# Sums of squares emitted a step behind their squares around an output projection, and two cache copies issued later

## The chip, the cores and the metric

The kernel runs on one core of a Trainium2 chip. It is measured in device microseconds (us) of one execution, lower being better. Five engines work side by side: TensorE (PE) multiplies matrices, VectorE (DVE) and ScalarE (ACT) work elementwise, GpSimd (POOL) does some elementwise work, and SyncE (SP) issues most DMAs. ACT issues some DMAs too. Each engine runs its own instructions in the order in which the program lists them, and waits on semaphores for the others.

## The reference

One inference step of one decoder layer, on a prompt of 1024 tokens and on 8 short sequences of 4 tokens (1056 columns in all, model width 1024, float32):

```python
h = rmsnorm(x, g_pre)
p = h @ w_in                       # split among three mixers and three gates
za, conv_a_new = causal_dwconv(a_c * a_in, conv_a_prev, conv_a_w)
ya = a_b * za                      # mixer A: gated convolution
yb, k_new, v_new = window_attn_...(q, k, v, ...)   # mixer B: window attention
yc = chunk_spatial_gate(c_u, rmsnorm(c_v, g_v), w_s, b_s)   # mixer C
g = sigmoid(gates)
merged = g[0] * (ya @ w_ba) + g[1] * (yb @ w_bb) + g[2] * (yc @ w_bc)
x = x + rmsnorm(merged @ w_o, g_post)
up = rmsnorm(x, g_pre_f) @ w_up
upc, ffn_new = causal_dwconv(up, ffn_prev, conv_f_w, conv_f_b)
fa, fb = split(upc, 2)
x = x + rmsnorm((silu(fa) * fb) @ w_down, g_post_f)
```

Here `rmsnorm(z, g)` is `z * rsqrt(mean(z*z) + eps) * g` over the 1024 features. The key and value caches of the short sequences are also returned, shifted by four rows: 124 old rows of each of 8 sequences are copied from input to output, for keys (`wk`) and values (`wv`).

## The kernel before

Features lie on the 128 partitions (8 tiles of 128, index `n`), tokens along the free axis. The 1056 columns are cut into three chunks `c` of 352 (`CW`). Every float32 product is made of three passes: an operand is split into a rounded part and a remainder (`copy` on ACT, line 91, then `sub` on DVE, line 97), and `products` multiplies hi by hi, hi by lo and lo by hi. Weights come by DMA on SP's queue into `raw` (three buffers), and are split into `wh`/`wl` or into a place in `Y`.

The program runs in this order. First the input `x` is loaded into `M`; for each chunk ACT squares it (`sq`, `acc`, line 434), DVE adds the squares, `rstd_of` multiplies the sum by `ones` on PE (`aux<-ones,acc`), POOL raises it to the power -1/2 (`rs`, line 311), PE spreads it over the partitions (line 320), and DVE and ACT make `H`, the normalized operand. Then come the input projections, the mixers, and the branch stage: eight branch tiles `n`, each with three products, whose results are multiplied by the gates `sig` (loaded back from DRAM into 12 buffers) in `evac_y`. Then the output projection, the feed-forward up projections, the down projections, and the end.

In the output projection the chunks come one after another. For each of the 8 tiles of a chunk, `evac_o` lets ACT store the product times a gain in `M` and square it; DVE adds the squares into `acc`. When a chunk is done, a generator `chain(c, ...)` does the rest of that chunk a step at a time, while PE works on the next chunk: `rstd_of(acc)`; then for the tiles in pairs a multiplication by `rs` and an addition of the input `xr` (both DVE, `M<-M,rs` and `M<-M,xr`), a DMA of the new `x` to DRAM (`x2d`), two squares on ACT (`acc2` for the first pair, `sq` for the others) and two additions into `acc2` on DVE; then `rstd_of(acc2)` and the splitting into `H`. PE's order is written out by hand for the whole kernel, and DVE's order for this stage is the order in which the code emits it (`manual_schedule`). The other engines are put in order by a scheduler that works with its own estimate of time.

In the trace the sum of `chain` is called `acc`, its squares `sq` and, for the third chunk, both are `cz`; the third chunk's first sum lies in `R`. A DMA uses one of eight semaphores in turn, and waits until the DMA that used it last has landed.

Of the kernel before, what the change touches and what calls it, by code (L numbers as in the profile page):

```python
# [17 lines left out]
P = 128  # L18
# [4 lines left out]
CW = 352  # L23
# [16 lines left out]
def body(tc, i, o):  # L40
# [3 lines left out]
    with top, tc.manual_schedule(engines={mybir.EngineType.PE}):  # L44
# [48 lines left out]
        def tt(out, a, b, op, eng=dve):  # L93
            return eng.tensor_tensor(out, a, b, op=op)  # L94
# [764 lines left out]
        with tc.tile_pool(name="pb", bufs=1) as pb:  # L859
            sig = {}  # L860

            def load_g(n):
                for b in (0, 2, 1):
                    for c in CHUNKS:
                        s = sig[b, n, c] = pb.tile([P, CW], F32, name="sig", tag="sig", bufs=12)
                        nc.sync.dma_start(s, sigd[:, 8 * b + n, cc(c)])

            def evac_y(b, n):
                def f(c, ps):
                    m, s = M8[:, n, cc(c)], sig.pop((b, n, c))  # L870
                    if b == 0:
                        tt(m, ps, s, ALU.mult)
                        return
                    tt(s, ps, s, ALU.mult)
                    last = tt(m, m, s, ALU.add, pool)
                    if n == 1 and b == 1 and c == 2:
                        with tc.issue_after(last.ins):
                            nc.scalar.dma_start(o["wk"], i["ck"][:, 4:, :])
                            nc.scalar.dma_start(o["wv"], i["cv"][:, 4:, :])
                    if b == 1:  # L880
                        copy(H[:, n, cc(c)], m)
                        sub(H[:, 8 + n, cc(c)], m, f32(H[:, n, cc(c)]))
                return f

            for n in range(8):
                load_g(n)
                unit(2, lambda k: Y[:, 12 + k, :], lambda k: Y[:, 14 + k, :], evac_y(0, n))
                unit(2, lambda k: Y[:, 8 + k, :], lambda k: Y[:, 10 + k, :], evac_y(2, n))
                unit(4, lambda k: Y[:, k, :], lambda k: Y[:, 4 + k, :], evac_y(1, n))
# [1 line left out]

        pcs = ExitStack()
        pc = open_pool(pcs, "pc", bufs=1)
        sums = {}

        def evac_o(n, acc):
            def f(c, ps):
                act.activation(M8[:, n, cc(c)], ps, AF.Identity, scale=g_post[:, n : n + 1])
                if c == 2:
                    if n == 0:  # L900
                        act.activation(acc, ps, AF.Square)
                        return
                    sq = pc.tile([P, CW], F32, name="sq", bufs=1)
                    act.activation(sq, ps, AF.Square)
                    tt(acc, acc, sq, ALU.add)
                elif n < 2:
                    act.activation(acc[:, n, :], ps, AF.Square)
                else:
                    if n % 2 == 0:
                        sums[c] = pc.tile([P, 2, CW], F32, name="sq2", bufs=1)  # L910
                    act.activation(sums[c][:, n % 2, :], ps, AF.Square)
                    if n % 2:
                        tt(acc, acc, sums[c], ALU.add)
            return f

        def load_xr(c, n, xr, queue=nc.sync):
# [2 lines left out]
        def chain(c, acc, rs, xr, acc2, sq, fill):  # L919
# [2 lines left out]
                return [None] * n  # L922

            queue = nc.sync if c < 2 else nc.scalar
            yield
            spread = rstd_of(acc, rs)
            next(fill, None)
            yield from wait(2)
            spread()
            for n in range(0, 8, 2):  # L930
                m = M8[:, n : n + 2, cc(c)]
                tt(m, m, rs.unsqueeze(1).to_broadcast([P, 2, CW]), ALU.mult)
                tt(m, m, xr[n // 2], ALU.add)
                queue.dma_start(x2d[:, n : n + 2, cc(c)], m)
                if c == 2 and n < 4:
                    load_xr(c, n + 4, xr[n // 2], queue)
                for q in range(2):
                    if n == 0:
                        act.activation(acc2[:, q, :], m[:, q, :], AF.Square)
                    else:  # L940
                        act.activation(sq[q], m[:, q, :], AF.Square)
                if n:
                    for q in range(2):
                        tt(acc2[:, q, :], acc2[:, q, :], sq[q], ALU.add)
                yield
            yield from wait(3)
            spread = rstd_of([acc2[:, 0, :], acc2[:, 1, :]], R[:, cc(c)])
            next(fill, None)
# [23 lines left out]
        for c in CHUNKS:  # L972
            if c < 2:
                xr = [pc.tile([P, 2, CW], F32, name="xr", bufs=4) for _ in range(4)]
                for n in range(0, 8, 2):
                    load_xr(c, n, xr[n // 2])
            acc = pc.tile([P, 2, CW], F32, name="acc") if c < 2 else R[:, cc(2)]
            for n in range(8):
                for _ in products(8, Hhi, Hlo, evac_o(n, acc), (c,), pieces=wow + 2 * n):
                    for step in steps:  # L980
# [4 lines left out]
            if c < 2:  # L985
                pair = lambda name, **kw: pc.tile([P, 2, CW], F32, name=name, **kw)
                sq = pair("sq3")
                steps.append(chain(c, acc, pc.tile([P, CW], F32, name="rs"), xr, pair("acc2"),
                                   [sq[:, 0, :], sq[:, 1, :]], iter(())))
        pcs.close()  # L990
        pw.close()
        taken[0] = upw + 8
# [332 lines left out]
```

## Time and profile before

| | |
|---|---|
| time, median of 3 runs (lowest, highest) | 1483.58 us (1479.41, 2008.34) |
| profiled execution, its own time | 1479.45 us |
| span of its core, first to last instruction | 1477.7 us |
| PE busy, share of the span | 1430.0 us, 97% |
| DVE, ACT, POOL busy | 61%, 45%, 17% |

The span is counted from the first instruction to the last. All places below are given in us from its start: the input phase up to about 48, the branch stage from about 545 to 642, the output projection from 642 to 745, the up projections from there on. PE is the engine that is busy nearly all the time, so a change of the time has to be looked for where PE stands still or is slow.

### The profile page before, as it was taken

How to read it: one execution, taken by the hardware profiler on the slowest of the kernel's cores; microseconds unless marked ns; L12 is line 12 of the kernel's file. 1: busy time of each engine (PE TensorE's matmuls, PEld its weight loads, DVE VectorE, ACT ScalarE, POOL GpSimd, SP SyncE). 2: the span in 40 equal slices, each digit the busy share in tenths (PEclk: the TensorE clock that was granted, in tenths of full speed). 3: DMA queues.
4: the chain of work that ended last, by engine and by line, in shares of the span. 5: the costliest groups of instructions: out<-in, count | busy, mean ns of one | idle time of the engine just before them, and what ended most of it. 6: DMA issues, size and time to landing. Idle time of an engine off the chain costs nothing.

```text
span 1477.7 us, 25715 instructions
## 1 busy us (share of the span) xinstructions
PE 1430.0 (97%) x10163; PEld 1419.4 (96%) x10163; DVE 903.0 (61%) x1615; ACT 659.0 (45%) x1347; POOL 248.4 (17%) x319
## 2 busy tenths in 40 slices
PE   4899999999999999999899999999999999999997
PEld 4899999999999989999899999999999999999997
DVE  6844445324777546655578877778777783453546
ACT  5444444435776322244446554455544574121333
POOL 2100000012455215520002212222122110000000
PEclk9999999999999999999999999999999999999999
DMA  6222333211001136643232222221222174231315
GB/s 232 77 90 98 103 109 110 92 48 44 30 23 44 60 107 186 189 140 108 82 110 73 78 75 82 85 87 66 72 84 77 54 259 152 73 109 44 86 38 154
DMA packets 77833, 141.40 MB, mean 96 GB/s; under 512 B 8256, under 2 KB 34816, under 8 KB 77696
## 3 DMA queue, kind: packets, MB, share of 16 engines
q1 hardware_dynamic: 64816, 110.77, 23.7%
q10 hardware_dynamic: 12896, 28.98, 5.2%
q8 instruction: 80, 1.31, 0.4%
q14 instruction: 41, 0.34, 0.1%
HBM read 105.58 MB, written 35.16 MB: 95 GB/s over the span
## 4 chain that ended last, share of the span: by engine, by line
PE 90%; DVE 4%; ACT 2%; issue 2%; POOL 1%; DMA 1%; ACTq 0%; SPq 0%; POOLq 0%; DVEq 0%
PE mm L100 54%; PE wb L100 20%; PE aux L100 13%; DVE M L94 1%; POOL rs L311 1%; PE sp L100 1%; ACT M L700 1%; PE aux L713 1%; DMA M<-in_x 1%; DVE M L694 0%; DMA raw<-in_wu 0%; DVE acc L94 0%; DVE Y L97 0%; ACT Y L91 0%; PE aux L320 0%
## 5 line engine op out<-in xcount | busy, mean ns | idle before, releaser
L100 PE MATMUL mm<-Y,wh 128*128 128x264 f32 (+1 forms) x1824 | 363.8, 295 | 0.0
L100 PE MATMUL mm<-H,wh 128*128 128x352 f32 (+1 forms) x1568 | 354.3, 313 | 1.5 <-DVE Y L97 0.9
L100 PEld LDWEIGHTS mm<-Y,wh 128*128 128x128 f32 x1824 | 292.6, 188 | 0.0
L100 PE MATMUL mm<-Y,wl 128*128 128x264 f32 (+1 forms) x912 | 269.4, 295 | 0.0
L100 PEld LDWEIGHTS mm<-H,wh 128*128 128x128 f32 x1568 | 261.6, 188 | 2.5 <-PE aux L100 1.1
L100 PE MATMUL mm<-H,wl 128*128 128x352 f32 (+1 forms) x784 | 243.7, 311 | 0.0
L100 PEld LDWEIGHTS mm<-Y,wl 128*128 128x128 f32 x912 | 171.8, 188 | 0.0
L100 PE MATMUL wb<-H,wh 128*128 128x264 f32 (+1 forms) x720 | 147.7, 298 | 0.0
L91 ACT ACTIVATE wh<-M 128x512 fp32r<-128x512 f32 x126 | 79.5, 631 | 152.8 <-PE aux L100 65.9
L100 PEld LDWEIGHTS mm<-H,wl 128*128 128x128 f32 x784 | 147.3, 188 | 0.0
L91 ACT ACTIVATE wh<-raw 128x512 fp32r<-128x512 f32 (+1 forms) x98 | 58.3, 594 | 169.2 <-PE mm L100 110.6
L1062 DVE SCALAR_TENSOR_TENSOR cz<-U,cst,cz 128x1072 f32<-128x1072 f32 x88 | 113.8, 1330 | 11.0 <-ACT cz L1060 11.0
L100 PEld LDWEIGHTS wb<-H,wh 128*128 128x128 f32 x720 | 116.4, 188 | 0.0
L100 PE MATMUL mm<-H,Y 128*128 128x352 f32 x624 | 107.2, 331 | 2.6 <-DVE H L97 2.6
L100 PE MATMUL wb<-H,wl 128*128 128x264 f32 (+1 forms) x360 | 107.3, 298 | 0.0
L97 DVE TENSOR_TENSOR wl<-M,wh 128x512 fp32r<-128x512 f32 x126 | 86.5, 686 | 32.8 <-ACT wh L91 32.8
L100 PEld LDWEIGHTS mm<-H,Y 128*128 128x128 f32 x624 | 103.1, 192 | 3.0 <-DVE H L97 3.0
L97 DVE TENSOR_TENSOR wl<-xraw,wh 128x512 fp32r<-128x512 f32 x70 | 48.5, 693 | 90.3 <-ACT wh L91 89.8
L311 POOL TENSOR_TENSOR rs<-rs,nhalf 88x4 f32<-88x4 f32 (+2 forms) x12 | 23.6, 1964 | 392.5 <-DVE rs L310 392.5
L94 DVE TENSOR_TENSOR M<-mm,M 128x352 f32<-128x352 f32 (+3 forms) x79 | 39.5, 506 | 76.2 <-PE mm L100 76.2
L94 DVE TENSOR_TENSOR M<-M 128x512 f32<-128x512 f32 (+1 forms) x88 | 69.5, 790 | 27.1 <-DMA M<-in_wu 26.3
L97 DVE TENSOR_TENSOR wl<-raw,wh 128x512 fp32r<-128x512 f32 (+1 forms) x72 | 53.0, 737 | 51.7 <-ACT wh L91 51.7
(222 smaller groups left out, 2635.8 us busy)
## 6 DMA issues: line engine op xcount, KB each, us to landing
M<-in_wu SPq DMA_DIRECT2D x72, 256.0 KB, 2.6
sig<-sigd SPq DMA_DIRECT2D x72, 176.0 KB, 2.9
y2d<-cz ACTq DMA_DIRECT2D x22, 528.0 KB, 2.8
sigd<-M ACTq DMA_DIRECT2D x40, 264.0 KB, 3.4
xraw<-in_win SPq DMA_DIRECT2D x40, 256.0 KB, 2.7
raw<-in_wd SPq DMA_DIRECT2D x40, 256.0 KB, 2.6
raw<-in_win SPq DMA_DIRECT2D x39, 256.0 KB, 2.6
Y<-y2d SPq DMA_DIRECT2D x14, 528.0 KB, 6.6
```

The source lines that it names most:

```text
L91: act.activation(out, in_, AF.Copy)
L94: return eng.tensor_tensor(out, a, b, op=op)
L97: eng.tensor_tensor(out, a, b, op=ALU.subtract)
L100: pe.matmul(out, lhsT, rhs, start=start, stop=stop, skip_group_check=more)
L311: pool.tensor_tensor(v, v, nhalf[:bs, :nb], op=ALU.pow)
L700: act.activation(s[:, h, :], s[:, h, :], AF.Exp, bias=ng[:, h : h + 1], scale=SCALE, accum_out=l[:, h : h + 1])
L713: pe.transpose(pt[:, h * P : (h + 1) * P], s[:, h, kb * P : (kb + 1) * P], ident)
L1062: dve.scalar_tensor_tensor(z, u[:, s : s + CONV], cwf[:, f, s : s + 1], z, ALU.mult, ALU.add)
```

## The change

It has two parts. In the output projection the addition of a square is not emitted next to the square any more but one step later: `evac_o` squares every tile by itself into one of three `sq` buffers, appends its addition to a list `late`, and first empties that list of the tile before (`flush`); `chain` adds the squares of a pair of tiles (`add_squares`) after the next pair's DVE work. The sum `acc` of the first two chunks is 352 wide, where it was two halves of 352 that were added up at the end. And the two DMAs that copy the cache rows are tied to the copy of branch tile 1 into `H` on ACT, where they were tied to an addition on POOL.

```diff
-                    last = tt(m, m, s, ALU.add, pool)
-                    if n == 1 and b == 1 and c == 2:
-                        with tc.issue_after(last.ins):
-                            nc.scalar.dma_start(o["wk"], i["ck"][:, 4:, :])
-                            nc.scalar.dma_start(o["wv"], i["cv"][:, 4:, :])
+                    tt(m, m, s, ALU.add, pool)
                     if b == 1:
-                        copy(H[:, n, cc(c)], m)
+                        last = act.activation(H[:, n, cc(c)], m, AF.Copy)
+                        if n == 1 and c == 2:
+                            with tc.issue_after(last.ins):
+                                nc.scalar.dma_start(o["wk"], i["ck"][:, 4:, :])
+                                nc.scalar.dma_start(o["wv"], i["cv"][:, 4:, :])
...
+        late = []
+
+        def flush():
+            while late:
+                tt(*late.pop())
 
         def evac_o(n, acc):
             def f(c, ps):
                 act.activation(M8[:, n, cc(c)], ps, AF.Identity, scale=g_post[:, n : n + 1])
...
+                if n == 0:
+                    act.activation(acc, ps, AF.Square)
+                    return
+                sq = pc.tile([P, CW], F32, name="sq", bufs=3)
+                act.activation(sq, ps, AF.Square)
+                flush()
+                late.append((acc, acc, sq, ALU.add))
             return f
...
             queue = nc.sync if c < 2 else nc.scalar
+            flush()
             yield
             spread = rstd_of(acc, rs)
...
+            def add_squares():
+                for q in range(2):
+                    tt(acc2[:, q, :], acc2[:, q, :], sq[q], ALU.add)
+
             for n in range(0, 8, 2):
...
+                if n > 2:
+                    add_squares()
                 for q in range(2):
-                    if n == 0:
-                        act.activation(acc2[:, q, :], m[:, q, :], AF.Square)
-                    else:
-                        act.activation(sq[q], m[:, q, :], AF.Square)
-                if n:
-                    for q in range(2):
-                        tt(acc2[:, q, :], acc2[:, q, :], sq[q], ALU.add)
+                    act.activation(sq[q] if n else acc2[:, q, :], m[:, q, :], AF.Square)
                 yield
+            add_squares()
```

PE and POOL keep their order; on ACT, DVE and SP it moves at the following places. At the head of ACT's program, before:

```order
L333 DMA cst<-in_cst 128x80
L91 ACT_TABLE_LOAD
L91 ACTIVATE warm<-nhalf 128x4
L878 DMA out_wk<-in_ck 8x15872
L879 DMA out_wv<-in_cv 8x15872
L91 ACTIVATE Y<-raw 128x512
L434 ACTIVATE acc<-M 128x704
```

and after, in the branch stage, where the next product's weights are split between the copies of a tile into `H`:

```order
L91 ACTIVATE wh<-raw 128x512
L877 ACTIVATE H<-M 128x352
L880 DMA out_wk<-in_ck 8x15872
L881 DMA out_wv<-in_cv 8x15872
L91 ACTIVATE wh<-raw 128x256 x2
```

The copies were ACT's fourth and fifth instruction, ahead of all work on `x`; now they stand behind the third `H<-M` of branch tile 1. The rest of the input phase has the same order on ACT.

DVE, while PE works on the third chunk and `chain` on the second, before (`acc_7599` is that chain's `acc2`, `R` the third chunk's first sum, `Y<-raw,Y` the splitting of weights for the up projections):

```order
L94 TENSOR_TENSOR M<-M,rs 128x2x352
L94 TENSOR_TENSOR M<-M,xr 128x2x352
L94 TENSOR_TENSOR acc_7599<-acc_7599,sq_7597 128x352 x2
L94 TENSOR_TENSOR R<-R,sq 128x352
L94 TENSOR_TENSOR M<-M,rs 128x2x352
L94 TENSOR_TENSOR M<-M,xr 128x2x352
L94 TENSOR_TENSOR acc_7599<-acc_7599,sq_7597 128x352 x2
L97 TENSOR_TENSOR Y<-raw,Y 128x512 x2
L94 TENSOR_TENSOR M<-M,rs 128x2x352
L94 TENSOR_TENSOR M<-M,xr 128x2x352
L94 TENSOR_TENSOR acc_7599<-acc_7599,sq_7597 128x352 x2
L94 TENSOR_TENSOR R<-R,sq 128x352
```

and after (`acc_7613` is the same sum):

```order
L94 TENSOR_TENSOR M<-M,rs 128x2x352
L94 TENSOR_TENSOR M<-M,xr 128x2x352
L94 TENSOR_TENSOR R<-R,sq 128x352
L94 TENSOR_TENSOR M<-M,rs 128x2x352
L94 TENSOR_TENSOR M<-M,xr 128x2x352
L94 TENSOR_TENSOR acc_7613<-acc_7613,sq_7611 128x352 x2
L97 TENSOR_TENSOR Y<-raw,Y 128x512 x2
L94 TENSOR_TENSOR M<-M,rs 128x2x352
L94 TENSOR_TENSOR M<-M,xr 128x2x352
L94 TENSOR_TENSOR acc_7613<-acc_7613,sq_7611 128x352 x2
L94 TENSOR_TENSOR R<-R,sq 128x352
L94 TENSOR_TENSOR acc_7613<-acc_7613,sq_7611 128x352 x2
```

Each pair of additions has moved behind the multiplication and addition of the next pair of tiles; the last two pairs of additions now stand next to each other, with one addition into `R` between them.

ACT at the same place, before:

```order
L941 ACTIVATE sq_7597<-M 128x352 x2
L898 ACTIVATE M<-mm,cst 128x352
L91 ACTIVATE Y<-raw 128x512
L941 ACTIVATE sq_7597<-M 128x352 x2
L91 ACTIVATE wh<-raw 128x512
```

and after:

```order
L941 ACTIVATE sq_7611<-M 128x352 x2
L902 ACTIVATE M<-mm,cst 128x352
L907 ACTIVATE sq<-mm 128x352
L91 ACTIVATE Y<-raw 128x512
L91 ACTIVATE wh<-raw 128x512
L941 ACTIVATE sq_7611<-M 128x352 x2
```

The last two squares of the chain stood behind one splitting of weights, and now stand behind two, and behind the square of the product that PE has just finished.

## Rows read from the trace of the kernel before

**Rows 1.** The page, busy time of each engine.

```profile
PE 1430.0 (97%) x10163; PEld 1419.4 (96%) x10163; DVE 903.0 (61%) x1615; ACT 659.0 (45%) x1347; POOL 248.4 (17%) x319
```

**Rows 2.** Waits of PE: us in total, times, longest.

```profile
PE aux L100 <- DVE acc L94: 19.7, 4, 14.5
```

**Rows 3.** Timeline, input phase: start, duration, engine, line, instructions, [idle before <-releaser].

```profile
0.81 0.40 SPq L135 DMA_DIRECT2D raw<-in_win  x1
...
1.34 1.26 ACTq L878 DMA_DIRECT2D out_wk<-in_ck  x1
...
4.03 0.63 ACT L91 ACTIVATE Y<-raw 128x512 fp32r<-128x512 f32 x1 [1.26 <-DMA raw<-in_win]
...
10.06 0.79 ACT L434 ACTIVATE acc<-M 128x704 f32<-128x704 f32 x1 [5.40 <-DMA M<-in_x]
...
12.58 0.79 ACT L434 ACTIVATE sq<-M 128x704 f32<-128x704 f32 x1 [0.16 <-DMA M<-in_x]
...
14.50 2.51 PE L100 MATMUL aux<-ones,acc 128*88 128x1 f32 x16 [14.50 <-DVE acc L94]
```

**Rows 4.** Busy time by stretch, ending with PE clock, DMA share, GB/s.

```profile
4.00:10.00 6.00, 0.00 (x0) 0.00 (x0) 0.86 (x2) 0.63 (x1) 0.00 (x0) 1.00 0.76 265
...
16.00:22.00 6.00, 3.74 (x24) 3.39 (x25) 4.68 (x9) 4.67 (x9) 1.66 (x1) 1.00 1.06 396
```

**Rows 5.** Waits of SP's queue in the input phase.

```profile
SPq L135 <- DMA out_wk<-in_ck: 1.8, 1, 1.8
```

**Rows 6.** Timeline of PE, output projection and first up projections.

```profile
691.72 1.51 PE L100 MATMUL aux<-ones,acc 128*88 128x1 f32 x16
...
707.41 0.76 PE L100 MATMUL aux<-ones,acc 128*88 128x1 f32 x8 [0.24 <-DVE acc L94]
708.03 4.11 PE L100 MATMUL wb<-H,Y 128*128 128x352 f32 x24
...
730.75 2.56 PE L100 MATMUL aux<-ones,acc 128*88 128x1 f32 x16 [4.68 <-DVE acc L94]
733.17 5.93 PE L100 MATMUL wb<-H,Y 128*128 128x352 f32 x24
...
768.18 1.64 PE L100 MATMUL aux<-ones,cz 128*88 128x1 f32 x16 [0.64 <-issue]
```

**Rows 7.** Busy time by stretch, behind PE's wait; PE clock third from the end.

```profile
731.00:738.00 7.00, 7.00 (x35) 7.00 (x35) 2.44 (x7) 2.64 (x5) 1.00 (x1) 0.56 0.25 75
```

**Rows 8.** Timeline of DVE while PE works on the third chunk.

```profile
717.78 0.89 DVE L94 TENSOR_TENSOR M<-M,xr 128x704 f32<-128x704 f32 x1
720.99 0.96 DVE L94 TENSOR_TENSOR acc<-acc,sq 128x352 f32<-128x352 f32 x2 [2.32 <-ACT sq L941]
721.87 0.52 DVE L94 TENSOR_TENSOR R<-R,sq 128x352 f32<-128x352 f32 x1
...
724.74 0.96 DVE L94 TENSOR_TENSOR acc<-acc,sq 128x352 f32<-128x352 f32 x2 [0.62 <-ACT sq L941]
725.62 1.29 DVE L97 TENSOR_TENSOR Y<-raw,Y 128x512 fp32r<-128x512 f32 x2
...
730.08 0.96 DVE L94 TENSOR_TENSOR acc<-acc,sq 128x352 f32<-128x352 f32 x2 [1.45 <-ACT sq L941]
```

**Rows 9.** Timeline of ACT at the same place.

```profile
729.03 0.63 ACT L91 ACTIVATE Y<-raw 128x512 fp32r<-128x512 f32 x1 [3.50 <-DMA raw<-in_wu]
729.57 0.87 ACT L941 ACTIVATE sq<-M 128x352 f32<-128x352 f32 x2
```

**Rows 10.** Timeline of SP's queue, branch stage and output projection.

```profile
571.87 1.62 SPq L866 DMA_DIRECT2D sig<-sigd  x3
...
726.37 0.96 SPq L135 DMA_DIRECT2D raw<-in_wu  x2
```

**Rows 11.** The tile sig in the branch stage: its loads, from issue to landing.

```profile
DMA to landing us min/median/max: 2.3/2.8/4.7
```

**Rows 12.** Timeline of DVE, start of branch tile 3: its second use of sig.

```profile
583.29 0.51 DVE L94 TENSOR_TENSOR M<-wb,sig 128x352 f32<-128x352 f32 x1
```

More of the change, by code (lines that the diff above doesn't have):

```diff
@@ L893, in body @@
         pc = open_pool(pcs, "pc", bufs=1)
-        sums = {}
+        late = []
+        def flush():
+            while late:
+                tt(*late.pop())
         def evac_o(n, acc):
@@ L898, in f @@
                 act.activation(M8[:, n, cc(c)], ps, AF.Identity, scale=g_post[:, n : n + 1])
-                if c == 2:
-                    if n == 0:
[L901 to L907, printed above, removed]
-                else:
[L909 to L913, printed above, removed]
+                if n == 0:
[5 more added lines that the diff above has]
+                late.append((acc, acc, sq, ALU.add))
             return f
@@ L936, in chain @@
                     load_xr(c, n + 4, xr[n // 2], queue)
+                if n > 2:
+                    add_squares()
                 for q in range(2):
-                    if n == 0:
-                        act.activation(acc2[:, q, :], m[:, q, :], AF.Square)
-                    else:
-                        act.activation(sq[q], m[:, q, :], AF.Square)
-                if n:
-                    for q in range(2):
-                        tt(acc2[:, q, :], acc2[:, q, :], sq[q], ALU.add)
+                    act.activation(sq[q] if n else acc2[:, q, :], m[:, q, :], AF.Square)
                 yield
+            add_squares()
             yield from wait(3)
@@ L976, in body @@
                     load_xr(c, n, xr[n // 2])
-            acc = pc.tile([P, 2, CW], F32, name="acc") if c < 2 else R[:, cc(2)]
+            acc = pc.tile([P, CW], F32, name="acc") if c < 2 else R[:, cc(2)]
             for n in range(8):
@@ L987, in body @@
                 sq = pair("sq3")
-                steps.append(chain(c, acc, pc.tile([P, CW], F32, name="rs"), xr, pair("acc2"),
+                steps.append(chain(c, [acc], pc.tile([P, CW], F32, name="rs"), xr, pair("acc2"),
                                    [sq[:, 0, :], sq[:, 1, :]], iter(())))
+        flush()
         pcs.close()
```

## The prediction, made before the result was known

> **What bounds the kernel now.** I read the page first: PE is busy 97% of the span and no other engine above 61% [rows 1]. Nothing that is saved on DVE or ACT counts by itself; only time in which PE stands still, or runs slowly, can be won or lost. The waits of PE name what it stands still for: one releaser holds most of it, DVE's `acc`, 19.7 us in four waits [rows 2]. The change touches exactly those sums, so I looked for the four. One is the head of the program, 14.50 us [rows 3], and its sum is that of the input phase, which the change does not edit; but it takes two DMAs away from there. The next in length is at 730.75, 4.68 us, in the output projection; a third, 0.24 us, is at 707.41 [rows 6]. A stall of 0.64 us at 768.18 is booked as issue, but stands before the same kind of sum, that of the third chunk [rows 6]. From the end of the input phase to the end PE is nearly gapless, so a us won before 48 or at these places should reach the end.
>
> **The copies, at the start.** The first DMA in the program is issued at 0.81 and its data is used at 4.03, 3.2 us later [rows 3]. The input's second piece follows it on the same queue within about 1 us, and would at the same delay be there at about 5. ACT gets to square it only at 10.06, having waited 5.40 us for that DMA, and the last piece of the chunk only at 12.58 [rows 3]. In between the DMA engines moved 265 GB/s, although work was queued; later, with the same queue of inputs, they move 396 [rows 4]. What else is on them is the two cache copies, issued from 1.34 on [rows 3], and one weight load waited 1.8 us for the semaphore that the first copy held [rows 5]. So the copies are in the way. What they cost I bound twice. From below: each is 496 KB, together 1.016 MB, and at 396 GB/s that many bytes take 2.6 us; that is what goes if the engines only have fewer bytes to move. From above: the first two pieces are there at 5.0 in place of 10.06, and the other three pieces of the chunk, 352 KB each, follow at 396 GB/s in 0.91 us each, the last at 7.7 in place of 12.58. Both give about 5.0. I take 5.0, because the wait that ends last is that of ACT for these pieces, and because the second of the two is held back longer than its own bytes and the copies' bytes take.
>
> Does this shift reach PE? ACT's last square, DVE's last addition and PE's first matmul at 14.50 follow each other without another wait, and from there the order on ACT and DVE is the same as before; the second chunk's pieces come after the first's at the same 396 GB/s, so they move by the same 5.0. Behind that stands a chain of DVE and POOL work that no DMA releases. I let all 5.0 us through.
>
> The Trainium skill, "DMA: Bandwidth & Descriptors", section "Issuing engines are not separate DMA queues", says that DMAs run on the same 16 engines and interleave with each other, whichever engine issued them. By it, moving the copies moves their cost with them into the branch stage, and the time would be that of the second rival below. The trace agrees about the start, where copies on ACT's queue hold up loads on SP's.
>
> **The copies, in the branch stage.** They now come behind ACT's copy of tile 1 into `H`, at about 571. Nothing in the trace shows them there; the nearest row is the start, where they held a load up by 5.0 us. A load of `sig` needs 2.8 us, 4.7 at most [rows 11], so it may now need some 8 to 10. The three loads issued from 571.87 [rows 10] are, counted from the first, the 29th to 31st; the 28th to 36th belong to branch tile 3, whose second use of `sig` starts at 583.29 [rows 12]. That is 11.4 us after the issue. So the lead covers the delay, and I cost the copies at nothing here. Uncovered they cost at most the same 5.0 us, since PE would wait as ACT did at the start. ACT's issuing of the first copy took 1.26 us [rows 3]; ACT is not the engine that sets the pace there.
>
> **The long stall of the output projection.** PE needs the second chunk's `acc2` and gets it at 730.75. On DVE three waits for squares stand before that: 2.32, 0.62 and 1.45 us, 4.39 in all [rows 8]. The change fills them. I redo DVE's row by hand in the new order, from the end of the second pair at 718.67 (717.78 and 0.89), where nothing has moved yet; neighbours overlap by some 0.08 us. One addition into `R` (0.52) until 719.1, the third pair's multiplication and addition (two of 0.89) until 720.9. Then the additions of the second pair's squares, which are there at 720.99 as before: until 721.95. So the third pair is through 3.2 us earlier. The splitting (1.29) lasts until 723.2, the fourth pair until 724.9, the third pair's additions until 725.8, `R` until 726.2. Now the last two additions need the last two squares, and these stand on ACT behind two splittings of weights. The first was held by its DMA until 729.03 [rows 9], issued at 726.37 [rows 10], 0.75 after DVE's splitting had begun at 725.62 [rows 8]; its way was 2.66. In the new order DVE's splitting begins at 721.9, so the DMA is issued at 722.6 and lands at 725.3, the second one 0.6 later at 725.9. ACT splits until 726.5, squares until 727.4, and DVE's additions run from about 726.9. PE started 0.67 after the start of these additions (730.08 to 730.75), so now at 727.5: 3.25 us earlier. What is late next is then that second weight load, and PE still stands 1.5 us.
>
> The 0.24 us at 707.41 goes too, since the addition of two halves (part of the sum that PE waits for) is gone. Together 3.5 us. From below: the last squares could be held as long as before, and nothing is won; from above the whole stall goes, 4.9 us.
>
> **The slow stretch behind the stall.** After the 4.68 us PE's granted clock averages 0.56 of full speed between 731 and 738 [rows 7], so mostly the lower of its levels, 1.2 GHz in place of 2.4. The sum's 16 matmuls take 2.56 us and 24 matmuls 5.93 [rows 6], where 1.51 and 4.11 are the rows at full clock [rows 6]: 1.05 and 1.82, 2.87 us lost. Behind 0.24 us of standing still the clock did not fall (4.11 at 708.03). A remaining stall of 1.5 lies between the two, nearer to the short one; I take the 2.87 as won, and zero as the other end.
>
> **The third chunk.** Its chain has the same order, and its stall of 0.64 shrinks; the last additions come by the same reckoning some 0.7 earlier. I take 0.5, between 0 and 0.64. The first chunk's sum at 691.72 has no stall to lose; its last additions are late at most by what is priced under the third rival.
>
> **Sum.** 5.0 + 3.5 + 2.9 + 0.5 = 11.9 us. The profiled execution took 1479.45 us (its span is 1477.7), so 1479.45 - 11.9 = **1467.6**. That execution is the lowest shown to within 0.1 us, and the median of the three is 4.1 above it, so the median of after can lie as far above.
>
> **Rivals.** First, the stall stays: the last squares stand behind two weight splittings in place of one, and these hang on DMAs that wait for DVE. For it: ACT's 3.50 us [rows 9] is the longest wait on that path. Against it: the DMAs' own release moves 3.7 us ahead. Only the start is won: 1479.45 - 5.0 = 1474.4.
>
> Second, what the copies give back at the start they take again in the branch stage, or the input phase does not follow the DMAs because DVE and POOL set its pace. Only the output projection is won: 1479.45 - 6.9 = 1472.6. Against it: the lead of 11.4 us.
>
> Third, slower: each chain's squares now wait for the additions of the pair before, which share one pair of buffers, so that ACT and DVE wait for each other in turn. At the end of a chain the additions of 0.96 lie ahead of the last squares, and ACT may put an evacuation and a splitting (about 1.0 and 0.6) between: 2.6 us. Where PE meets a chain's sum, at 691.72, 730.75 and 768.18, it would stand 2.6 longer, 7.8 in all, and one more stall of the long kind brings another 2.9 of slow clock: 10.7 lost, less the 5.0 of the start, 1479.45 + 5.7 = 1485.1. It decides from 1.7 us a chain on (three times 1.7 is 5.0). Against it: by the reckoning above DVE has 1.8 us of other work between a pair's squares and their additions.
>
> **How the numbers follow.** Forecast 0.65; first rival 0.13; second 0.14; third 0.05; something else 0.03. Within the forecast the start may give 2.6 to 5.0 or a little more, the projection 4 to 8.4: 1465 to 1473, and the median's own scatter adds up to 4. The first two rivals lie inside or next to that. The range is 1462 to 1477. About 2% (29.7 us) is what a measurement of this kernel can tell from no change, and no case comes near that: faster by over 2% 0.02, within 2% 0.95, slower by over 2% 0.03.
>
> **What would show it.** Start: ACT's first square of `x` at about 5 in place of 10.06, PE's first sum at about 9.5 in place of 14.50, and DMA at full rate throughout. Branch stage: no wait of DVE or ACT for a DMA behind the copies. Output projection: PE's stall before `acc2` of the second chunk at 1 to 2 us, the 24 matmuls behind it at 4.1, ACT's longest wait now before a splitting of weights. I am wrong if PE's first sum moves by much less than 5 us, if the clock still falls behind the shorter stall, or if a new wait of PE appears between 571 and 600.

## The result, and the profile after

| | before | after |
|---|---|---|
| median | 1483.59 us of 4 | 1472.26 us of 4 (1469.69 to 1473.37) |
| profiled execution, span | 1479.45, 1477.7 | 1473.37, 1471.0 |
| ratio, 95% interval | | 0.9931 (0.9905 to 0.9956) |

The ratio leaves out the execution of before that took 2008.34. It stands for 10.2 us (6.5 to 14.1); the forecast was 1467.6, with 1462 to 1477 as its range. The two profiled executions are 6.1 us apart, less than the ratio says, since before's lies near the lowest of its kernel and after's is the highest of its four. The sum of the prediction, 11.9, was made against the first of them. Where the difference comes from can be read by taking the same matmul in both traces, since PE's order is the same. First PE's waits for `acc` (us in total, times, longest), which answer to [rows 2]:

```profile
PE aux L100 <- DVE acc L94: 13.8, 3, 10.6
```

Of four waits three are left, and the longest has gone from 14.5 to 10.6. The input phase after, ACT and then PE (start, duration, engine, line, instructions, [idle before <-releaser]), against [rows 3]:

```profile
4.07 0.63 ACT L91 ACTIVATE Y<-raw 128x512 fp32r<-128x512 f32 x1 [1.30 <-DMA raw<-in_win]
5.31 0.79 ACT L434 ACTIVATE acc<-M 128x704 f32<-128x704 f32 x1 [0.61 <-DMA M<-in_x]
...
8.81 0.79 ACT L434 ACTIVATE sq<-M 128x704 f32<-128x704 f32 x1 [0.18 <-DMA M<-in_x]
```

```profile
10.61 2.51 PE L100 MATMUL aux<-ones,acc 128*88 128x1 f32 x16 [10.61 <-DVE acc L94]
...
43.74 0.85 PE L320 MATMUL aux<-ident,rs 88*128 88x88 f32 x4 [4.41 <-POOL rs L311]
```

The first square is at 5.31 in place of 10.06, and the sum at 10.61 in place of 14.50: 3.9 earlier. At 43.74, where before had 47.52 with the same wait of 4.41, 3.8 are left, so nothing is lost on the way, although the second chunk's sum moved by less (from 20.11 to 16.74, 3.4) and PE waited 1.43 for it where it had waited 0.27. Busy time by stretch after (PE's granted clock is third from the end):

```profile
4.00:10.00 6.00, 0.00 (x0) 0.00 (x0) 2.99 (x5) 4.02 (x6) 0.00 (x0) 1.00 1.03 332
43.00:50.00 7.00, 6.26 (x23) 6.26 (x24) 4.88 (x9) 1.44 (x2) 0.68 (x1) 0.51 0.00 0
446.00:450.00 4.00, 4.00 (x19) 4.00 (x18) 1.78 (x5) 2.25 (x10) 0.70 (x2) 0.58 0.00 0
729.00:736.00 7.00, 7.00 (x37) 6.97 (x37) 2.32 (x6) 3.13 (x6) 0.39 (x1) 0.76 0.14 52
```

The DMA engines now move 332 GB/s where it was 265 [rows 4]. But behind the wait of 4.41 us PE ran at 0.51 of its clock for the whole stretch (before: 0.76 in 47 to 54), and around 446, behind a wait of 1.89 that both traces have, at 0.58, where before had 1.00. By the starts of the same matmuls these two stretches cost 1.3 and 1.5 us more than they did before. Of the 3.9 won at the start only 1.0 arrives at the output projection: its first sum is at 690.71, before at 691.72 [rows 6]. The rest of PE there:

```profile
705.89 0.76 PE L100 MATMUL aux<-ones,acc 128*88 128x1 f32 x8
706.51 4.13 PE L100 MATMUL wb<-H,Y 128*128 128x352 f32 x24
...
726.31 1.60 PE L100 MATMUL aux<-ones,acc 128*88 128x1 f32 x16 [1.80 <-DVE acc L94]
727.78 5.66 PE L100 MATMUL wb<-H,Y 128*128 128x352 f32 x24
...
761.75 1.34 PE L100 MATMUL aux<-ones,cz 128*88 128x1 f32 x16
```

The stalls of 0.24 and 0.64 are gone, and that of 4.68 is 1.80. The lead over before grows from 1.0 to 1.5, 4.4 and 6.4, and the spans are 6.7 apart. Behind the long stall 16 and 24 matmuls take 1.60 and 5.66, against 2.56 and 5.93 before and 1.51 and 4.11 at full clock [rows 6]: of 2.87 us of slow clock 1.23 are won and 1.64 stay. What PE waited for, DVE and then ACT, against [rows 8, 9]:

```profile
723.20 0.95 DVE L94 TENSOR_TENSOR acc<-acc,sq 128x352 f32<-128x352 f32 x2
724.07 0.52 DVE L94 TENSOR_TENSOR R<-R,sq 128x352 f32<-128x352 f32 x1
725.64 0.96 DVE L94 TENSOR_TENSOR acc<-acc,sq 128x352 f32<-128x352 f32 x2 [1.06 <-ACT sq L941]
```

```profile
723.50 0.64 ACT L91 ACTIVATE Y<-raw 128x512 fp32r<-128x512 f32 x1
724.60 0.63 ACT L91 ACTIVATE wh<-raw 128x512 fp32r<-128x512 f32 x1 [0.46 <-DMA raw<-in_wu]
725.13 0.87 ACT L941 ACTIVATE sq<-M 128x352 f32<-128x352 f32 x2
```

DVE's three waits of 4.39 us are one of 1.06, and ACT's 3.50 for a weight load is 0.46. The load of the second weights is still among what comes last, but with 0.46 us; the rest of the 1.80 is, by these rows, ACT's two splittings themselves and DVE's own row; an experiment below tests that.

### The profile page after: what moved, and what is told of

It reads as the page before. It is cut to its first block, busy times and chain, and to the rows that moved or that the text cites. A ratio compares the mean times of both kernels' runs of the same rounds, so it can differ in the third digit from the quotient of the medians.

```text
span 1471.0 us, 25720 instructions
## 1 busy us (share of the span) xinstructions
PE 1430.5 (97%) x10163; PEld 1420.2 (97%) x10163; DVE 901.8 (61%) x1621; ACT 659.1 (45%) x1347; POOL 246.9 (17%) x319
## 4 chain that ended last, share of the span: by engine, by line
PE 90%; DVE 3%; ACT 2%; issue 2%; DMA 2%; POOL 1%; SPq 0%; POOLq 0%; DVEq 0%; ACTq 0%
PE mm L100 54%; PE wb L100 20%; PE aux L100 13%; POOL rs L311 1%; DVE M L94 1%; DMA M<-in_x 1%; PE sp L100 1%; ACT M L700 1%; PE aux L713 1%; DVE M L417 1%; DVE M L694 0%; DMA raw<-in_wu 0%; DVE Y L97 0%; DVE H L97 0%; DMA raw<-in_wo 0%
```

## The experiments

Every kernel was timed next to the kernel before on the same chip; a ratio is that of the two, with its 95% interval.

**The two parts by themselves.** The kernel before with the copies moved (as in the diff of the change), and the changed kernel with the copies where they were (the diff is the second's, against the changed kernel):

```diff
-                        last = act.activation(H[:, n, cc(c)], m, AF.Copy)
-                        if n == 1 and c == 2:
+                    last = tt(m, m, s, ALU.add, pool)
+                    if n == 1 and b == 1 and c == 2:
...
```

> The kernel before with the two cache copies moved, and nothing else. Theory (the copies hold back the pieces of x at the start): PE's first sum of squares at about 10.6 in place of 14.50, as in the changed kernel, everything behind it 3.8 us earlier; in the output projection the stalls of the kernel before stay (0.24, about 4.7 and 0.64 us) with a slow stretch behind the long one. 1483.6 - 3.8 = about 1480, or up to 1481.5 if the clock falls for longer behind the input phase, as it did in the changed kernel (half clock for 6.83 us in place of 3.41). Rival (the whole gain of the start is given back, by the copies' own cost in the branch stage or by the clock): 1483 to 1484, with a wait of PE, DVE or ACT for a DMA behind 571, or longer stretches at half clock.

> The changed kernel with the two cache copies left at the start, where they were. Theory (the two parts are independent): the input phase is that of the kernel before, PE's first sum at 14.50; in the output projection the stalls of 0.24 and 0.64 us are gone, the long one is 1.8 in place of 4.68, and the time is 1.5 + 2.9 + 1.2 + 0.3 = 5.9 us shorter: 1477.7; if the clock doesn't fall behind 1.8 us, another 1.7 shorter: 1476. Rival (what the changed kernel won in the projection came in part from the copies, through the place of the loads): the long stall is 3 us or more and the time 1480 or above.

Copies alone: 1476.45 median of 7, ratio 0.9961 (0.9947 to 0.9975), so 5.8 us, more than the 3.8 expected. Sums alone: 1477.13 of 9, 0.9955 (0.9941 to 0.9970), so 6.7 us. PE with the copies moved alone, then with the sums alone:

```profile
11.44 2.50 PE L100 MATMUL aux<-ones,acc 128*88 128x1 f32 x16 [11.44 <-DVE acc L94]
...
728.47 2.56 PE L100 MATMUL aux<-ones,acc 128*88 128x1 f32 x16 [4.66 <-DVE acc L94]
730.89 6.01 PE L100 MATMUL wb<-H,Y 128*128 128x352 f32 x24
```

```profile
16.38 2.51 PE L100 MATMUL aux<-ones,acc 128*88 128x1 f32 x16 [16.38 <-DVE acc L94]
...
730.07 2.49 PE L100 MATMUL aux<-ones,acc 128*88 128x1 f32 x16 [2.19 <-DVE acc L94]
732.42 6.35 PE L100 MATMUL wb<-H,Y 128*128 128x352 f32 x24
```

The parts are independent as far as this can tell: each changes its own place and leaves the other as it was, and together they give about what they give apart (12.5 us, with some 3 of uncertainty, against 10.2). With the sums alone the long stall is 2.19 and the clock behind it as slow as behind 4.68 (2.49 and 6.35 for the 16 and 24 matmuls), so there nothing of the slow stretch was won. With the same order as before, the first sum came at 16.38 here, not at 14.50: what the copies cost differs from one execution to the next.

**The copies in the branch stage.** Their two DMAs left out of the changed kernel:

> The changed kernel without the two cache copies: the outputs wk and wv are not written. Theory (the lead of 11 us hides the copies in the branch stage): the same time as the changed kernel, 1472.3 to within 1 us, and the same waits. Rival (the copies take again in the branch stage what they gave back at the start): up to 3.8 us less, 1468.5, with a shorter wait of DVE for sig and no change anywhere else.

1471.15 of 6, ratio 0.9921 (0.9905 to 0.9937), against 0.9931 and, below, 0.9924 with them. The times alone leave some 3 us open; the traces are sharper. From the end of the input phase to the output projection (43.74 to 690.71 with the copies, 43.59 to 690.24 without) PE needs 646.97 and 646.65 us, 0.3 apart, and the rival of 3.8 falls. In the changed kernel a load of `sig` needed up to 7.9 us to land in place of 4.7 [rows 11], and the lead of 11.4 us covered it, as reckoned. But PE at the long stall showed something else:

```profile
725.95 1.60 PE L100 MATMUL aux<-ones,acc 128*88 128x1 f32 x16 [1.85 <-DVE acc L94]
727.40 4.11 PE L100 MATMUL wb<-H,Y 128*128 128x352 f32 x24
```

The same stall, 1.85 us, and full clock behind it.

**The changed kernel again.**

> The changed kernel itself, a second time, beside the others. If what the clock loses behind the same stalls is chance, the stall of 1.8 us at the second chunk's sum comes back but the half clock behind it, and the one near 446, need not; the median lies at 1471 to 1473.5. If they belong to the kernel, both come back at the same places and for as long.

1471.70 of 6, ratio 0.9924 (0.9900 to 0.9948). The stall was 2.21, the 24 matmuls took 5.65, and the clock fell near 446 again, but behind the input phase it averaged 0.79 in 42 to 50, where the first run had 0.57, and PE waited 3.82 for POOL in place of 4.41. Nothing comes back exactly, so a profile's slow stretches are partly chance. The times say the same: the six executions ranged from 1465.69 at a mean clock of 0.995 to 1472.92 at 0.992.

**The chain alone.** Copies moved, `add_squares` a step behind as in the change, and `evac_o` and `acc` as before (two halves, squares added two at a time):

> Copies moved and only the chain's additions put a step later; the squares of the output tiles are summed as in the kernel before (two at a time, in two halves). Theory (the long stall belongs to the chain alone): the stall of 0.24 us at the second chunk's first sum stays, the long stall is 1.8 to 2.2 as in the changed kernel, the third chunk's 0.64 is gone, and the time is that of the changed kernel plus 0.3: 1472.5. Rival (the single addition in place of a pair is what lets DVE finish early): the long stall is 3 us or more, and the time 1474 to 1476.

1471.47 of 6, ratio 0.9927 (0.9905 to 0.9949): the time of the changed kernel. The stalls were 0.24, 2.13, and none at the third chunk. As far as the times can tell, all that the second part wins comes from the chain; putting the squares of the output tiles a step behind takes away the 0.24 us, which is below that.

**The rest of the long stall.** First PE was given more work ahead of the sum:

```diff
             add_squares()
-            yield from wait(3)
+            yield from wait(4)
```

> The changed kernel with wait(4) in place of wait(3) ahead of the second sum of each chain, so that PE does 12 more matmuls (about 2.05 us) before it needs the sum. Theory (1.80 us of standing still are left at that sum, and the clock falls behind them): the stall before the second chunk's sum is 0 to 0.2, the 24 matmuls behind it take 4.1 in place of 5.66, and the time is 1.8 + 1.2 to 1.5 = 3.0 to 3.3 us shorter: about 1469. Rival 1 (the clock falls at about this place whatever the stall is): 1.8 shorter, 1470.5. Rival 2 (the operand H of the chunk comes 2 us later and the up projections now wait for it): a new wait of PE for DVE or ACT behind the transposes, at 735 to 765, and a time of 1472 or more.

1475.39 of 7, ratio 0.9955 (0.9940 to 0.9970): slower than the changed kernel. PE:

```profile
708.05 0.76 PE L100 MATMUL aux<-ones,acc 128*88 128x1 f32 x8 [1.85 <-DVE acc L94]
708.67 5.66 PE L100 MATMUL wb<-H,Y 128*128 128x352 f32 x24
...
730.20 1.60 PE L100 MATMUL aux<-ones,acc 128*88 128x1 f32 x16
731.66 4.13 PE L100 MATMUL wb<-H,Y 128*128 128x352 f32 x24
...
745.69 0.76 PE L100 MATMUL aux<-ones,R 128*88 128x1 f32 x8 [1.82 <-DVE R L94]
746.31 5.65 PE L100 MATMUL mm<-H,Y 128*128 128x352 f32 x24
```

The stall at 730 is gone and the clock behind it full, but the chain's splitting into `H` came later on DVE, and the first sums of the next chunk stand behind it: two stalls of 1.8 us for one. The second rival had named the time and the place of the second stall (735 to 765), but for another operand; neither had named the first. Then the splittings of weights were put off, one output tile later each from the third on:

```diff
-                if c == 2 and n < 4:
-                    limit[0] = upw + 2 * n + 2 if n < 3 else 1 << 30
+                if c == 2 and n in (0, 1, 3, 4):
+                    limit[0] = {0: upw + 2, 1: upw + 4, 3: upw + 6, 4: 1 << 30}[n]
```

> The changed kernel with two of the four places at which weights for the up projections are split put one output tile later, so that DVE's and ACT's splittings no longer stand between the chain's last additions and squares. Theory (the remaining 1.80 us are DVE's splitting of 1.28 ahead of the fourth pair and ACT's second splitting ahead of the last squares): the fourth pair starts 1.2 us earlier on DVE, the last two squares at about 723.5 in place of 725.13, the additions end at 724.9, and PE's stall at the second chunk's sum is 0 to 0.4 us; 1.4 to 1.8 us shorter than the changed kernel, and up to 1.7 more in the executions in which the clock fell behind it: 1469 to 1471. Rival (the work that is put off is late next, at the third chunk's first sum near 743 or at the up projections' weights): a new stall of 1 us or more behind 727, and the time of the changed kernel, 1472 to 1473.

1473.11 of 6, ratio 0.9936 (0.9912 to 0.9960), no better than the changed kernel. PE:

```profile
717.57 1.60 PE L100 MATMUL aux<-ones,acc 128*88 128x1 f32 x16
...
724.01 0.49 PE L320 MATMUL aux<-ident,ru 88*128 88x88 f32 x4 [0.85 <-DVE ru L314]
...
735.42 0.76 PE L100 MATMUL aux<-ones,R 128*88 128x1 f32 x8 [1.19 <-DVE R L94]
...
754.52 1.64 PE L100 MATMUL aux<-ones,cz 128*88 128x1 f32 x16 [0.42 <-issue]
```

The stall went, as the theory had it, and 0.85, 1.19 and 0.42 came in its place, 2.46 for 1.80: the rival. So the splittings were indeed what made up the 1.80, but DVE has no free place for them nearby. This profiled execution had no slow stretch before its last 10 us and took 1466.43; the three at a mean clock of 0.992 took 1474 to 1475. But it is also the one in which the stall behind the input phase nearly vanished, though the edit doesn't touch it: PE waited 0.86 us for POOL there, where the changed kernel waited 4.41. The last section comes back to this.

**Why the copies cost so much at the start.** Twice the kernel before with other rows, first

```diff
-  nc.scalar.dma_start(o["wk"], i["ck"][:, 4:, :])
+  nc.scalar.dma_start(o["wk"].rearrange("b (q r) d -> b q (r d)", q=4), i["ck"][:, 4:, :].rearrange("b (q r) d -> b q (r d)", q=4))
```

(and the same for `wv`), then with `q b (r d)` as the order.

> The kernel before, copies at the start as they were, but each written as 32 rows of 15.9 KB in place of 8 of 63.5 KB: the same bytes, at the same place in ACT's program. Theory (a piece of x waits behind long rows of the copies on the DMA engines that carry them): the pieces of x come earlier, PE's first sum between the 10.6 to 11.4 seen without copies and the 14.5 to 16.4 seen with them, at about 12 to 13, and the time is 1.5 to 3 us shorter: about 1481. Rival (only the copies' bytes count, 2.6 us at 396 GB/s, or the order of the queues): the first sum at 14.5 or later, and 1483.

> The kernel before with the copies at the start, as 32 rows of 15.9 KB like the attempt with short rows, but in an order in which neighbouring rows don't lie next to each other, since there the trace still had packets of 63 KB (176 packets on that queue in both). Theory (a piece of x waits behind long packets on the engines that carry them): more packets on the queue, DMA share between 4 and 10 us at 0.9 or above in place of 0.76, ACT's first square at 6 to 8 and PE's first sum at 12 to 13, 2 to 3 us less than before. Rival (the copies cost their bytes and their place in the queues, whatever the packets): the first sum at 14.5 to 16.7, as in the three profiles with copies at the start, and no change of the time.

The first: 1482.71 of 12, ratio 1.0008 (0.9993 to 1.0024), first sum at 16.71. It tells nothing on rows, since the copies still went out in the same packets; the row of their queue (packets, MB, share), to 16 us, has the 176 packets of before, here and then in the second kernel:

```profile
q10 hardware_dynamic: 176, 1.06, 18.0%
```

```profile
q10 hardware_dynamic: 216, 1.06, 17.0%
```

The second: 1484.68 of 12, ratio 1.0020 (1.0005 to 1.0034), first square at 12.16 and first sum at 19.32, later than ever. Its busy time by stretch:

```profile
4.00:10.00 6.00, 0.00 (x0) 0.00 (x0) 0.87 (x2) 0.63 (x1) 0.00 (x0) 1.00 0.85 279
10.00:16.00 6.00, 0.00 (x0) 0.00 (x0) 0.00 (x0) 1.24 (x2) 0.00 (x0) 1.00 0.47 168
```

So shorter packets did not bring the first sum forward. But bytes alone don't explain it either: the engines were half idle from 10 to 16 while ACT waited for pieces of `x`.

The packets in the kept traces show what does. With the copies at the start, their 16 packets of 63,488 bytes are under way at most eight at a time, one for each row of a copy, in two rounds of about 2.5 us; they begin at 3.6 to 3.8 and end at 9.40 in the trace of before, at 10.98 with the sums alone and at 11.31 in the first of these kernels, and PE's first sum follows the end of the last one by 5.1 to 5.4 us. In the second kernel a copy's outer level has only four rows, its 64 packets of 15,872 bytes of 0.6 us run some four at a time until 14.71, and the first sum follows by 4.6. So the copies last 5.8 to 7.6 us, and then 11.3, where their bytes at 396 GB/s would take 2.6, and the last pieces of the chunk come behind them. That each copy holds as many of the 16 engines as it has rows is a reading of these traces; no copy that goes out as 16 rows or more tests it. And since the second kernel changed the number under way as well as the length of the packets, the length by itself stays untested.

Then the copies were issued in the input phase, behind the first chunk:

```diff
-                        act.activation(sq, M8[:, k : k + 2, cc(c)], AF.Square)
+                        last = act.activation(sq, M8[:, k : k + 2, cc(c)], AF.Square)
+                        if c == 0 and k == 6:
+                            with tc.issue_after(last.ins):
+                                nc.scalar.dma_start(o["wk"], i["ck"][:, 4:, :])
+                                nc.scalar.dma_start(o["wv"], i["cv"][:, 4:, :])
...
```

> The kernel before with the two copies still in the input phase, but put behind ACT's last square of the first chunk of x, so that they are issued at about 9.5 us, when the pieces of that chunk have landed. Theory (the copies cost what they do because they are issued ahead of the pieces that everything waits for): PE's first sum at 10.6 to 11.4 as without copies; the pieces of the second and third chunk and the first weights come up to 2.6 us later, the copies' bytes at 396 GB/s, and part of that shows as a longer wait of PE ahead of the second chunk's sum; 1477 to 1480, between the kernel with the copies moved to the branch stage (1476.45) and the kernel before. Rival (wherever the copies lie in the input phase, they hold later loads as long as they held the first): the second chunk's sum 4 us or more later than with the copies moved, and 1481 to 1483.

1480.0 of 12, ratio 0.9981 (0.9963 to 1.0000). PE:

```profile
10.92 2.51 PE L100 MATMUL aux<-ones,acc 128*88 128x1 f32 x16 [10.92 <-DVE acc L94]
...
21.38 2.50 PE L100 MATMUL aux<-ones,acc 128*88 128x1 f32 x16 [5.76 <-DVE acc L94]
```

The first sum is as early as without copies, and the second chunk's sum is 4.1 us later than with the copies moved away (17.25): the rival's number, in the profile, while the time is the upper end of the theory's. By the ratio 2.8 of the 5.8 us are still won. What counts is whether someone waits for a load while the copies run, not their order alone. Here too their packets run eight at a time, from 12.93 to 18.43, 5.5 us.

**The stall behind the input phase.** The slow clock that took back part of the gain follows PE's wait of 4.41 us for POOL, and there POOL's power of 88x4 elements took 5.93 us in the changed kernel, where in the output projection it took 1.01. One edit on the changed kernel lets DVE wait for POOL at that place (line 314 copies the result), and puts the work that filled DVE behind it:

```diff
-                dve.tensor_copy(u, v)
+                hold.append(dve.tensor_copy(u, v))
...
+                def held():
+                    hold[0] = True
+                    start(2)
+                    hold[0] = False
+
-                first(0, [lambda: end(1), lambda: start(2), lambda: end(2)])
+                first(0, [lambda: end(1), held, lambda: end(2)])
...
-            drain(combos(M8, 0))
+            with tc.issue_after(hold[1].ins):
+                drain(combos(M8, 0))
```

> The changed kernel with one edit in the input phase: behind the third chunk's sum DVE copies POOL's result (one 88x4 copy) before it goes on, and the work that fills DVE there is put behind that copy. In the changed kernel POOL's power of 88x4 took 5.93 us while DVE was busy without a gap, and PE stood 4.41 us for it, with half clock for 3.4 to 6.8 us behind. Theory (POOL is slow there because DVE leaves it no gap, and the clock falls because PE stands): POOL takes 1.5 to 3 us, PE stands at most 2 us there, the clock falls for 3.4 us or not at all, and the time is 2.4 to 5 us shorter than the changed kernel: 1467 to 1469.5. Rival 1 (POOL is slow for a reason of its own): the same 4.4 us, and 1472. Rival 2 (the work put back on DVE is late for the products behind): a new wait of PE for DVE between 45 and 60, and 1471 to 1474.

> The edit of the third sum in the input phase and the later splittings of weights together, on the changed kernel. Theory (each takes away one place where the clock can fall, and the two don't touch each other): no fall of the clock behind the input phase for more than 3.4 us, none at 727, and 1465 to 1468. Rival (what is won by fewer stalls is lost at other places, as the splittings put off alone gave 1473.1 against 1471.7): 1470 to 1473, with half clock recorded at places that had none.

The edit alone: 1467.34 of 5 (1465.03 to 1468.18), ratio 0.9898 (0.9882 to 0.9913), the best of all. With the splittings put off: 1468.08 of 4, 0.9904 (0.9890 to 0.9919), which adds nothing: as its rival had it, half clock came up at new places, for instance behind a wait of 0.48 us on PE:

```profile
754.50 1.65 PE L100 MATMUL aux<-ones,cz 128*88 128x1 f32 x16 [0.48 <-issue]
756.01 5.65 PE L100 MATMUL mm<-H,Y 128*128 128x352 f32 x24
```

POOL, PE and a stretch of the edit alone:

```profile
36.31 2.39 POOL L311 TENSOR_TENSOR rs<-rs,nhalf 88x4 f32<-88x4 f32 x1 [6.91 <-DVE rs L310]
```

```profile
39.56 0.49 PE L320 MATMUL aux<-ident,ru 88*128 88x88 f32 x4 [0.52 <-DVE ru L314]
39.84 8.02 PE L100 MATMUL wb<-H,Y 128*128 128x352 f32 x48
```

```profile
42.00:50.00 8.00, 8.00 (x52) 8.00 (x51) 8.00 (x13) 4.79 (x7) 0.00 (x0) 1.00 0.14 52
```

PE stands 0.52 us in place of 4.41, and the clock stays at 1.00 where the changed kernel had 0.57 in the same stretch. The median is 4.4 to 4.9 below the changed kernel's two. The intervals of the ratios just meet, but the nine executions with this edit lie between 1465.03 and 1469.25, and of the ten of the changed kernel only two lie below 1469. The long stall was 2.35 us in this trace, and the clock fell behind it (0.76 in 720 to 727), as in the changed kernel.

## Why the prediction was right, and what in it was not

**The start** (5.0 taken, 2.6 to 5.0): right, at the upper bound. The profiled pair shows 3.9, but before's 14.50 was an early one. Over the three profiles with the copies in their old place and form (14.50, 16.38, 16.71) the first sum is at 15.86 on the mean, over the nine with the copies out of the input phase (10.19 to 11.89) at 10.95: 4.9 us. The time of the copies alone, 5.8 (3.7 to 7.9), agrees. The lower bound, 2.6, reckoned the copies at 396 GB/s; in the traces with them at the start they lasted 5.8 us and more. The pieces of `x` did not quite follow at 0.91 us each, though: the last was squared at 8.81, not 7.7, and the second chunk's sum moved by 3.4, not by as much as the first.

**The shift reaching PE**: right to the end of the input phase, and then part of it was lost where the prediction had not looked. PE's wait of 4.41 for POOL stayed, and the clock behind it was lower for longer. The prediction's "so a us won before 48 or at these places should reach the end" left this out: a gain eaten by a stretch of slow clock elsewhere, worth 1.3 us there and 1.5 near 446 in the profiled pair. That it is partly chance the second run of the changed kernel showed.

**The branch stage** (nothing): right, by the kernel without copies; a `sig` load took up to 7.9 us there, and the lead of 11.4 covered it. The Trainium skill's rule ("DMA: Bandwidth & Descriptors", section "Issuing engines are not separate DMA queues") that DMAs from any engine interleave on the same 16 agrees with these 7.9 us; the lead decides whether it costs.

**The long stall** (3.25 of 4.68, 1.5 left): right in mechanism. 1.80 to 2.35 were left in six profiles with the new chain, so 2.3 to 2.9 won. The second weight load, named as late next, held only 0.46 of it; the splittings on ACT and DVE made the rest, as putting them off showed.

**The slow stretch** (2.87, all won): this is the step that failed. "A remaining stall of 1.5 lies between the two, nearer to the short one", it said, and so took the clock as full. It fell behind 1.80, 2.13, 2.19, 2.21 and 2.35; behind 1.85 it fell in one trace and not in another. In the profiled pair 1.23 was won, in one case all but 0.1, with the sums alone nothing. The prediction read the fall off the length of the stall, and that does not decide it: in two other traces the clock fell behind waits of 0.48 and 0.65 us (24 matmuls took 5.65 and 5.64), where it had stood behind 0.64 in before (4.13). What does decide it stays open. The value lay between the ends that the prediction kept, and it had named this as a way to be wrong.

**The third chunk** (0.5): the 0.64 is gone. The squares waiting for the additions of the pair before, the third rival, did show in the third chunk's chain: between 690 and 775 ACT waits twice for DVE's `cz`, 3.7 us in all and 2.0 at most, which before does not have. PE does not stand for it, as the row at 761.75 without a wait shows.

With the terms as the profiled pair has them, 3.9 + (0.24 + 2.88) + 1.23 + 0.6 = 8.9 less 1.3 and 1.5 gives the 6.1 by which the times differ. That it meets them is partly luck: the spans, which the traces cover, differ by 6.7. The terms leave out what the sums' own matmuls became shorter by (1.34 for 1.51 and for 1.64), and 0.6 of the difference of the spans is lost outside them. The profiled execution is 5.8 above the forecast: 2.8 is slow clock that was not foreseen, 1.6 slow clock that was taken as won, 1.1 the start, 0.4 the long stall, and the third chunk was 0.1 better. The prediction also took 2% as what can be told from no change; the interval of the ratio shows that 0.7% was clear of it.

## What to carry to other kernels

Where one engine is busy 97% of the time, look for what it stands still for, and count the slow clock behind a stall with the stall: the same wait of 4.41 us cost 1.3 us more in one execution than in another, and the edit against it was worth nearly half of the whole change. Here an addition that waits for another engine's square did better a step later in the order, and a copy that nobody waits for did better in a stage in which loads have a lead, not merely behind the first loads. Reckon the time of such a copy from its packets in the trace, and how many are under way at once, not from its bytes alone. Shifting work by one step can move a stall to the next sum instead of removing it, so follow the engine's row to the next place where someone waits.

## What the hardware showed that was not expected

POOL's power of 88x4 elements takes 1.00 to 1.02 us when DVE is idle, and up to 7.41 when it isn't. In the changed kernel the third one began at 37.76 and took 5.93; POOL and then DVE:

```profile
37.76 5.93 POOL L311 TENSOR_TENSOR rs<-rs,nhalf 88x4 f32<-88x4 f32 x1 [8.08 <-DVE rs L310]
```

```profile
40.98 1.24 DVE L97 TENSOR_TENSOR Y<-M,Y 128x1056 fp32r<-128x1056 f32 x1
42.14 0.68 DVE L94 TENSOR_TENSOR xraw<-xraw 128x512 f32<-128x512 f32 x1
45.12 1.08 DVE L417 SCALAR_TENSOR_TENSOR M<-M,cst,R 128x352 f32<-128x352 f32 x2 [2.30 <-ACT R L91]
```

DVE's row ends at 42.82, and POOL ends at 43.69, 0.87 later. In the trace of the best kernel DVE ran out at 37.83, with 0.82 us to wait for ACT, and POOL ended at 38.70: 0.87 again. DVE's copy stood later still, at 39.26, so it was not the copy that let POOL in.

A gap that can be seen is not needed, though. With the splittings put off, DVE has the order of the changed kernel here and no gap, and POOL still took only 2.39; POOL, DVE and PE:

```profile
38.95 2.39 POOL L311 TENSOR_TENSOR rs<-rs,nhalf 88x4 f32<-88x4 f32 x1 [8.08 <-DVE rs L310]
```

```profile
38.80 1.67 DVE L97 TENSOR_TENSOR H<-M,H 128x704 fp32r<-128x704 f32 x2
40.40 0.68 DVE L97 TENSOR_TENSOR wl<-xraw,wh 128x512 fp32r<-128x512 f32 x1
```

```profile
41.40 0.52 PE L320 MATMUL aux<-ident,rs 88*128 88x88 f32 x4 [0.86 <-POOL rs L311]
```

POOL ends at 41.34, 0.87 behind DVE's 40.47, and the next DVE instruction starts as closely as its neighbours. But that instruction had only just been released: ACT's splitting `wh`, which it reads, ended at 40.33. In the second run of the changed kernel (5.32, ending 0.87 behind 42.47) it was a DMA that landed 0.1 us before the next DVE instruction. In the other twelve traces this power ended 0.86 to 0.88 behind an instruction of DVE with 0.8 us or more of idle time after it. So the stall behind the input phase comes and goes with the timing of DVE's neighbours, also without the edit. That the faster executions of the changed kernel (1465.69 and 1467.06) are those in which POOL got in early is likely, but not shown, since they have no trace.

The Trainium skill ("SBUF — State Buffer", section "SBUF: two separate sides") says that the two engines share a pair of ports as an exclusive lock, held for a whole instruction by whoever starts first; for a DVE instruction with two inputs in SBUF, as `H<-M,H` has, it says so against a POOL instruction that reads SBUF. The traces agree that POOL stands back; that it mostly did not get in between six DVE instructions in a row either, only these runs show.
